# Where the weights start in SBUF: a shift of 0 to 96 bytes for each projection of a transformer block

## The chip, the cores and the metric

The kernel runs on one core of a Trainium2 chip. The metric is the device time of one execution in microseconds (us), as the median of several runs. The profile is of one execution of its own; its engines are TensorE (PE, and PEld for its weight loads), VectorE (DVE), ScalarE (ACT), GpSimd (POOL) and SyncE (SP, which issues DMAs).

## The reference

One block of a transformer on 256 tokens of 1024 features, in float32: a mixer and a feed-forward part, each behind a root-mean-square norm. The mixer joins 512 columns of attention (8 heads of 64, one block of 256 keys, so plain causal attention with a relative bias) with 512 of a gated causal convolution of 31 taps.

```python
u = rms_norm(h, mix_norm_g[l])
proj = u @ w_in[l]                                   # 1024 -> 5 * 512
q, k, v, glu_a, glu_g = jnp.split(proj, splits, axis=-1)
attn_out = moba_attention(heads(q), heads(k), heads(v), rel_bias)
conv_out = conformer_conv(glu_a, glu_g, ...)          # a * sigmoid(g), 31 taps, layer norm, silu
h = h + jnp.concatenate([attn_out, conv_out], -1) @ w_out[l]
u = rms_norm(h, ffn_norm_g[l])
h = h + (jax.nn.silu(u @ w_gate[l]) * (u @ w_up[l])) @ w_down[l]   # 2816 wide
return rms_norm(h, final_norm_g)
```

## The kernel before

Each large product is made of three matmuls on float32r operands. A weight tile raw (128 partitions x 1024 columns, 4 KB a partition) is loaded by SP; ScalarE casts it to the upper part wh, VectorE subtracts to get the rest, wl; x times its gain is cut the same way into uh and ul, the halves of u2. Then wh with uh, wh with ul and wl with uh are added in PSUM. The division by the norm is done behind the matmuls.

`high` allots wh and wl for each half n of a part, from the pool `wts` with 9 buffers for each of the tags raw (6), wh and wl. The parts' names begin with a letter: a (a and gate of the convolution), qk, v, o (output), g and u (gate and up, two 256-column halves side by side), d (down).

A matmul has a stationary operand, which a weight load (LDWEIGHTS, 128 columns) puts into the array, and a moving one. In the stages a, qk and o the weights are stationary and u2 (in o the mixer's result mh, ml) moves, 256 columns at a time. In v and gate/up, u2 is stationary and the weights move, 512 columns at a time; in down fh and fl (the feed-forward values) are stationary and the weights move. So each matmul reads one slice of a weight tile and one slice of another tile at the same time as the weight load of the next one.

Counts: a and gate 192 (`a_mm`, tiles pa and pg), queries and keys 192 (`qk_mm`, `mm3`, pqk), values 48 (`v_mm`, pv), output 192 (`o_part`, py), gate/up 528 (`up_mm`, pf), down 252 and 24 narrower ones at the end (`down`, pd and pe): 1428 of these matmuls.

The order of the work is written out by hand: PROGRAM lists the steps of the mixer, and the loop over 11 groups g at the end of the kernel those of the feed-forward part. Everything is kept in program order on each engine. The stages stand in this order: a0 and a1 (a and gate), with the sum of squares of x (`rs`: ps_x) among them; then queries and keys, attention's scores, the convolution (pc, in plain float32) and values interleaved; then output with the layer norm of the convolution's result among it (`norm`, parts 1, 2, 6, 3, 7, 4, 5); then gate/up and down in turn.

Tiles lie in SBUF one behind another in the order in which pools and tiles are made, each rounded up to 32 bytes. mhalf, of which two columns are used, is made first with 24 floats (96 bytes), so xs and u2 start 96 bytes past a multiple of 128. The 16 spare floats of pv put ones and ident at 0 and, further on, every raw, wh and wl at 96 past a multiple of 128. accx (96 past) and rbt (32 bytes) stand first in the pool w1; behind them the mixer's tiles, mh and ml among them, start at a multiple of 128. In the pool w2 the feed-forward part's tiles, fh and fl among them, start at 96 past one.

Of the kernel before, what the change touches and what calls it, by code (L numbers as in the profile page):

```python
# [10 lines left out]
F32 = mybir.dt.float32  # L11
F32R = mybir.dt.float32r
AF = mybir.ActivationFunctionType
ALU = mybir.AluOpType

P = 128
S = 256
D = 1024
KD = D // P
H = 8  # L20
HD = 64
NB = 32
TAPS = 31
CC = 4
# [6 lines left out]
ZN = 384  # L31
HW = 1024
# [4 lines left out]
FINE = ("a0_0", "a0_4")  # L37
COPY_V = (("a0_0", 0), ("a0_0", 1))
WARM = 9

PROGRAM = """
ld.a1_0 a0.0 pz a0.1 a0.2 a0.3 zs zd ld.a1_1 a0.4 a0.5 a0.6 a0.7 ld.qk0
# [13 lines left out]
PV_N = PV_FOLD + 32  # L56
# [3 lines left out]
def block_kernel(ctx, tc, xT, w_in, w_out, w_gu, w_down, pvec, gfin, relb, hot, out):  # L60
    nc = tc.nc
    const = ctx.enter_context(tc.tile_pool(name="const", bufs=1))
    wts = ctx.enter_context(tc.tile_pool(name="wts", bufs=9))
# [3 lines left out]
    w1 = ph1.enter_context(tc.tile_pool(name="w1", bufs=1))  # L67
# [3 lines left out]
    def mm(*args, **kw):  # L71
        return tc.keep_in_program_order(nc.tensor.matmul(*args, **kw))  # L72
# [12 lines left out]
    act, vec, pool, sync = (InOrder(e) for e in (nc.scalar, nc.vector, nc.gpsimd, nc.sync))  # L85

    def bank(i, name):
        return psum.tile([P, 512], F32, tag=f"b{i}", name=name)
# [17 lines left out]
    def pieces(name):  # L106
        n = HW // 2 if name in FINE else HW
        return [(i, slice(j, j + n)) for i in range(2) for j in range(0, HW, n)]
# [12 lines left out]
    def take(name):  # L121
        if name[0] in "gud" and name not in ("g0", "u0", "g1"):
            while order and len(raws) < 1 + LOOK:
                fetch(order[-1][2])
        return raws.pop(name)
# [5 lines left out]
    def high(name, i):  # L131
        if i == 0:
            raw = take(name)
            upper[name] = []
            parts[name] = []
            for n in range(2):
                wh = wts.tile([P, HW], F32R, tag="wh", name=f"wh_{name}_{n}")
                wl = wts.tile([P, HW], F32R, tag="wl", name=f"wl_{name}_{n}")
                parts[name].append((wh, wl))
                upper[name] += [(raw[n], wh, wl, c) for m, c in pieces(name) if m == n]  # L140
        raw, wh, wl, c = upper[name][i]
        if (name, i) in COPY_V:
            vec.tensor_copy(wh[:, c], raw[:, c])
        else:
            act.copy(wh[:, c], raw[:, c])
        made.add((name, i))
# [3 lines left out]
    def split(name, i=None):  # L150
        for n in range(len(pieces(name))) if i is None else (i,):
            if (name, n) not in made:
                high(name, n)
            raw, wh, wl, c = upper[name][n]
            vec.tensor_sub(wl[:, c], raw[:, c], wh[:, c].bitcast(F32))
# [10 lines left out]

    mhalf = const.tile([P, 24], F32, name="mhalf")
    xs = const.tile([P, KD, S], F32, name="xs")  # L170
    u2 = const.tile([P, KD, 2, S], F32R, name="u2")
    uh, ul = u2[:, :, 0], u2[:, :, 1]
    pv = const.tile([P, PV_N + 16], F32, name="pv")
    ones = const.tile([P, P], F32, name="ones")
    ident = const.tile([P, P], F32, name="ident")
    warm = const.tile([P, 1], F32, name="warm")
    accx = w1.tile([P, S], F32, name="accx")
    rbt = w1.tile([NB + 1, H], F32, name="rbt")
    hot_s = w1.tile([NB + 1, ZN], F32, name="hot_s", tag="lg", bufs=2)
    upad = [w1.tile([P, 2 * UW + 4], F32, name=f"upad{i}", tag="pts", bufs=4) for i in range(2)]  # L180
    ustk = []
    wstk = [w1.tile([P, 8 * Q, 32], F32, name=f"wstk{i}", tag="wstk", bufs=2) for i in range(2)]
    invc = w1.tile([P, P], F32, name="invc")
    vec.memset(warm, 0.0)
    act.dma_start(pv[:, 0:PV_T], pvec[:, 0:PV_T])
    act.activation(warm, warm, AF.Sigmoid)
# [3 lines left out]
        sync.dma_start(xs[:, k], xT[:, k * S : (k + 1) * S])  # L190
    pool.memset(ones, 1.0)
    pool.dma_start(hot_s, hot)
    pool.dma_start(rbt[0:NB, :], relb)
    wm = bank(4, "wm")
    for i in range(WARM):
        mm(wm[:, 0:P], ones, ones, start=i == 0, stop=i == WARM - 1)
    pool.memset(ident, 0.0)
    pool.affine_select(out=ident, in_=ident, compare_op=ALU.not_equal, fill=1.0, base=0,
                       pattern=[[-1, P]], channel_multiplier=1)
    pool.memset(mhalf, -0.5)  # L200
    pool.memset(rbt[NB : NB + 1, :], 1.0)
    for t in upad:
        pool.memset(t[:, 0 : TAPS - 1], 0.0)
        pool.memset(t[:, TAPS - 1 + S : UW + TAPS - 1], 0.0)
        pool.memset(t[:, UW + TAPS - 1 + S :], 0.0)
    pool.memset(invc, 1.0 / (CC * P))
    pool.dma_start(pv[:, PV_T:PV_N], pvec[:, PV_T:])

    col = lambda lo, i: pv[:, lo + i : lo + i + 1]
# [11 lines left out]
    def rstd(acc, n, eps, name, b):  # L221
        ps = bank(b, f"ps_{name}")
        for t in range(2):
            mm(ps[:, t : t + 1], acc[:, t * P : (t + 1) * P], ones[:, 0:1], start=True, stop=True)
        ms = const.tile([P, 2], F32, name=f"ms_{name}")
        vec.tensor_scalar(ms, ps[:, 0:2], 1.0 / n, eps, op0=ALU.mult, op1=ALU.add)
        rc = const.tile([P, 2], F32, name=f"rc_{name}")
        pool.tensor_tensor(rc, ms, mhalf[:, 0:2], op=ALU.pow)
        dg = const.tile([P, S], F32, name=f"dg_{name}", tag="dg")
        for t in range(2):  # L230
            vec.tensor_scalar(dg[:, t * P : (t + 1) * P], ident, rc[:, t : t + 1], None, op0=ALU.mult)
        return rc, dg

    def wide(dg, name, b):
        pb = bank(b, f"pb_{name}")
        mm(pb[:, :S], ones, dg, start=True, stop=True)
        return pb
# [22 lines left out]
    cv = lambda c: cacc[:, c]  # L260
# [75 lines left out]
    def scale_x():  # L336
        xn["c"], xn["d"] = rstd(accx, D, RMS_EPS, "x", 5)
# [16 lines left out]
    pzs = []  # L354

    def bias_mm():
        pzs.append(bank(6, "pz"))
        mm(pzs[0][0:H, 0:ZN], rbt, hot_s, start=True, stop=True)

    def bias_copy():  # L360
        act.copy(zs, pzs[0][0:H, 0:ZN])
# [120 lines left out]
    s4 = w1.tile([P, 2, S], F32, name="s4")  # L482
    ln = {}

    def norm(part):
        if part == 1:
            vec.tensor_add(s4[:, 0], s4[:, 0], s4[:, 1])
        elif part == 2:
            pm = bank(2, "pm")
            mm(pm[:, :S], invc, s4[:, 0], start=True, stop=True)  # L490
            for c in range(CC):
                vec.tensor_sub(cv(c), cv(c), pm[:, :S])
        elif part == 6:
            csq.append(w1.tile([P, CC, S], F32, name="csq", tag="wstk", bufs=2))
            for c in range(CC):
                act.activation(cw(c), cv(c), AF.Square)
        elif part == 3:
            vec.tensor_add(s4[:, 0], cw(0), cw(1))
            vec.tensor_add(s4[:, 1], cw(2), cw(3))
            vec.tensor_add(s4[:, 0], s4[:, 0], s4[:, 1])  # L500
        elif part == 7:
            _, ln["dg"] = rstd(s4[:, 0], CC * P, LN_EPS, "ln", 4)
        elif part == 4:
            ln["r"] = wide(ln["dg"], "ln", 5)
        else:
            for c in range(CC):
                vec.tensor_mul(cv(c), cv(c), ln["r"][:, :S])
                act.activation(cw(c), cv(c), AF.Silu, scale=col(PV_LG, c), bias=col(PV_LB, c))
                act.copy(mix[0][:, 4 + c], cw(c))
            for c in range(CC):  # L510
                vec.tensor_sub(mix[1][:, 4 + c], cw(c), mix[0][:, 4 + c].bitcast(F32))


    acch = const.tile([P, S], F32, name="acch")

    def finish(m):
        assert len(done) == KD - 3
# [7 lines left out]
    def a0(k):  # L525
        high(f"a0_{k // 4 * 4}", k % 4)
        upper_u(k, PV_G1)
        lower_u(k, PV_G1)
        split(f"a0_{k // 4 * 4}", k % 4)
        a_mm(0, k, f"a0_{k // 4 * 4}", k % 4 * 512)  # L530

    ops = {"ld": fetch, "zd": bias_out, "bd": bias_in, "ud": stack_out, "us": stack_in, "h": high, "w": split, "rb": row_scale, "pz": bias_mm, "zs": bias_copy, "vt": v_out, "rs": scale_x,
           "a0": a0, "a1": a1, "glu": glu, "qk": qk_mm, "qo": qk_out, "sc": score, "t": logits, "n": normed, "fl": flip,
           "fo": flip_out, "v": v_mm, "pv": pv_mm, "mo": mix_out, "l": norm, "o": o_mm, "f": finish, "c": conv,
           "co": conv_out, "cw": conv_weights, "ct": conv_taps, "hs": lambda m: sumsq(acch, xs[:, m], m, "h"),
           "sq": lambda k: sumsq(accx, xs[:, k], k, "x"), "g": lambda m: lower_u(m, PV_G2)}
# [96 lines left out]
    for k in range(KD):  # L633
        for t in range(2):
            up_mm(0, t, k)
        if k == 5:
            rc2, _ = rstd(acch, D, RMS_EPS, "h", next(spare))
            split("u1")
# [38 lines left out]
    a, b = FG - 2, FG - 1  # L677
    for t in range(2):
# [22 lines left out]
        ms = w2.tile([P, 2], F32, name=f"fms{t}")  # L701
        for n, (lo, hi) in enumerate(((512, 768), (768, 1024))):
# [5 lines left out]
            if n == 0:  # L708
# [4 lines left out]
                                 op0=ALU.mult, op1=ALU.add, accum_out=ms[:, 1:2])  # L713
# [97 lines left out]
```

## Time and profile before

| | us |
|---|---|
| median of 3 runs | 298.7 (298.55 to 298.9) |
| the profiled execution | 298.79 |
| its span (first to last instruction of the profile) | 297.0 |
| TensorE busy in the span | 289.4 (97%) |
| VectorE, ScalarE, GpSimd busy | 203.9, 149.7, 44.3 |

The page gives busy times of each engine and a chain of work followed back from the end. Matmuls overlap: one lasts longer than the time from its start to the start of the next, so the busy time of a group is less than its count times its mean. The chain in order of time gives the start and length of each piece with the count of matmuls in it, and the quotient is the time from start to start.

### The profile page before, as it was taken

Reading aid. Unit: us, or ns where it says so; the run is one execution under the profiler, and the core shown is the slowest. Engines: PE = TensorE matmul, PEld = TensorE weight load, DVE = VectorE, ACT = ScalarE, POOL = GpSimd, SP = SyncE. Lnnn points to the kernel's source line nnn. Section 1 sums busy time; section 2 is a strip of 40 time slices with the busy share of each in tenths; the row PEclk is TensorE's granted clock in tenths of the full one; section 3 lists DMA queues with packets and bytes.
Section 4 is the critical chain, followed back from the end, with each engine's and each line's share of the span. In section 5 each row is a group of like instructions: output and inputs, shape, how many; then the busy total and the mean of one; then the engine's idle time right before and its main releaser. Section 6 shows DMA issues by size and latency. Waiting matters only on the chain.

```text
span 297.0 us, 4763 instructions
## 1 busy us (share of the span) xinstructions
PE 289.4 (97%) x1750; PEld 246.9 (83%) x1750; DVE 203.9 (69%) x373; ACT 149.7 (50%) x251; POOL 44.3 (15%) x83
## 2 busy tenths in 40 slices
PE   8999999999999999999999999999999999999991
PEld 7999986988689998888888888888888888888880
DVE  2877999888988688867875738291847456321884
ACT  2984564354583768826555445271717263402531
POOL 4000000000000000124131303320421313130000
PEclk9999999999999999999999999999999999999996
DMA  6999779936227445797997968979694959520012
GB/s 182 344 406 335 251 170 261 382 94 195 74 73 225 142 144 200 244 354 228 307 348 168 310 166 275 303 259 374 222 282 134 297 144 311 165 71 0 1 68 75
DMA packets 21624, 63.73 MB, mean 215 GB/s; under 512 B 3117, under 2 KB 5701, under 8 KB 21600
## 3 DMA queue, kind: packets, MB, share of 16 engines
q1 hardware_dynamic: 18176, 54.80, 57.2%
q0 software_dynamic: 2992, 8.08, 9.8%
q10 hardware_dynamic: 432, 0.54, 0.5%
q8 instruction: 14, 0.23, 0.3%
q14 instruction: 10, 0.08, 0.1%
HBM read 58.08 MB, written 5.32 MB: 213 GB/s over the span
## 4 chain that ended last, share of the span: by engine, by line
PE 92%; issue 2%; DMA 2%; DVE 1%; SPq 0%; POOLq 0%; POOL 0%; ACT 0%; DVEq 0%
PE pf L72 40%; PE pd L72 17%; PE pqk L72 8%; PE py L72 8%; PE pv L72 4%; PE pa L72 4%; PE pg L72 4%; PE pc L72 4%; DMA xs<-in_xT 2%; PE ps L72 1%; PE pt L75 1%; PE po L72 1%; DVE ht L83 1%; SPq L83 0%; DVE hg L83 0%
## 5 line engine op out<-in xcount | busy, mean ns | idle before, releaser
L72 PE MATMUL pf<-wh_u,u 128*128 128x512 f32 x176 | 56.2, 390 | 0.0
L72 PE MATMUL pf<-wh_g,u 128*128 128x512 f32 x176 | 55.9, 389 | 0.0
L83 DVE TENSOR_TENSOR ff<-fs,pf 128x256 f32<-128x256 f32 x22 | 9.1, 420 | 53.4 <-ACT fs L83 53.4
L83 ACT ACTIVATE fs<-pf,rc_h 128x256 f32<-128x256 f32 x22 | 10.4, 476 | 65.9 <-PE pf L72 65.4
L72 PEld LDWEIGHTS pf<-wh_u,u 128*128 128x128 f32 x176 | 33.0, 188 | 6.8
L72 PEld LDWEIGHTS pf<-wh_g,u 128*128 128x128 f32 x176 | 33.0, 188 | 6.8
L72 PE MATMUL pf<-wl_g,u 128*128 128x512 f32 x88 | 34.2, 389 | 0.0
L72 PE MATMUL pf<-wl_u,u 128*128 128x512 f32 x88 | 34.2, 389 | 0.0
L72 PE MATMUL pd<-wh_d,fh 128*128 128x512 f32 x84 | 32.9, 391 | 0.0
L72 PE MATMUL pd<-wh_d,fl 128*128 128x512 f32 x84 | 32.7, 390 | 0.0
L72 PE MATMUL pd<-wl_d,fh 128*128 128x512 f32 x84 | 32.7, 389 | 0.0
L83 DVE TENSOR_TENSOR wl_u<-raw_u,wh_u 128x1024 fp32r<-128x1024 f32 x22 | 26.6, 1223 | 7.5 <-ACT wh_u L83 7.4
L83 POOL DMA_DIRECT2D fb<-fd x40 | 23.2, 588 | 46.5 <-DMA fd<-fv 22.8
L83 ACT CAST wh_u<-raw_u 128x1024 fp32r<-128x1024 f32 x22 | 22.9, 1053 | 12.5 <-PE pf L72 9.2
L83 DVE TENSOR_TENSOR wl_g<-raw_g,wh_g 128x1024 fp32r<-128x1024 f32 x22 | 25.9, 1221 | 2.0 <-ACT wh_g L83 2.0
L83 DVE TENSOR_TENSOR wl_d<-raw_d,wh_d 128x1024 fp32r<-128x1024 f32 x22 | 25.6, 1205 | 0.5 <-ACT wh_d L83 0.5
L72 PE MATMUL pqk<-u,wh_qk 128*128 128x256 f32 x128 | 23.6, 286 | 0.0
L83 ACT CAST wh_g<-raw_g 128x1024 fp32r<-128x1024 f32 x22 | 22.0, 1049 | 0.0
L83 ACT CAST wh_d<-raw_d 128x1024 fp32r<-128x1024 f32 x22 | 21.9, 1045 | 0.0
L72 PEld LDWEIGHTS pqk<-u,wh_qk 128*128 128x128 f32 x128 | 20.0, 192 | 0.4 <-issue 0.3
L72 PEld LDWEIGHTS pf<-wl_u,u 128*128 128x128 f32 x88 | 16.5, 188 | 3.4
L72 PEld LDWEIGHTS pf<-wl_g,u 128*128 128x128 f32 x88 | 16.5, 188 | 3.4
(156 smaller groups left out, 558.4 us busy)
## 6 DMA issues: line engine op xcount, KB each, us to landing
raw_g<-in_w_gu SPq DMA_DIRECT2D x22, 512.0 KB, 5.6
raw_u<-in_w_gu SPq DMA_DIRECT2D x22, 512.0 KB, 7.0
raw_d<-in_w_down SPq DMA_DIRECT2D x22, 512.0 KB, 4.7
raw_qk<-in_w_in SPq DMA_DIRECT2D x8, 512.0 KB, 7.2
raw_o<-in_w_out SPq DMA_DIRECT2D x8, 512.0 KB, 4.2
fd<-fv POOLq DMA_DIRECT2D x10, 256.0 KB, 4.0
fb<-fd POOLq DMA_DIRECT2D x40, 64.0 KB, 5.8
ustk<-ud SPq DMA_DIRECT2D x8, 288.0 KB, 5.7
```

The lines of the kernel that those rows point to most:

```text
L72: return tc.keep_in_program_order(nc.tensor.matmul(*args, **kw))
L75: return tc.keep_in_program_order(nc.tensor.transpose(o, i, ident))
L83: return lambda *a, **k: tc.keep_in_program_order(f(*a, **k))
```

## The change

Every slot of wh and wl becomes 32 floats (128 bytes) longer, and the part lies in it s floats from the start: 24 (96 bytes) for a and gate, 16 (64 bytes) for queries, keys, values and down, 8 (32 bytes) for output, 0 for gate and up. mhalf moves behind ident and shrinks to 8 bytes, pv's padding from 16 to 8 floats, rbt is widened to 128 bytes and accx and acch become one tile, acc, in the first pool. With that xs, u2, raw, all slots of wh and wl, fh and fl start at a multiple of 128 bytes; mh and ml stay at one. hg and fsq, at the end, start 32 bytes past one.

The tile invc (all 1/512) goes: the mean over the convolution's channels is now made with ones, and the division is done in the subtraction.

```diff
+SHIFT = {"a": 24, "q": 16, "o": 8, "v": 16, "d": 16}
+
...
             for n in range(2):
-                wh = wts.tile([P, HW], F32R, tag="wh", name=f"wh_{name}_{n}")
-                wl = wts.tile([P, HW], F32R, tag="wl", name=f"wl_{name}_{n}")
+                s = SHIFT.get(name[0], 0)
+                wh, wl = (wts.tile([P, HW + 32], F32R, tag=w, name=f"{w}_{name}_{n}")[:, s : s + HW] for w in ("wh", "wl"))
                 parts[name].append((wh, wl))
...
-    mhalf = const.tile([P, 24], F32, name="mhalf")
+
     xs = const.tile([P, KD, S], F32, name="xs")
     u2 = const.tile([P, KD, 2, S], F32R, name="u2")
     uh, ul = u2[:, :, 0], u2[:, :, 1]
-    pv = const.tile([P, PV_N + 16], F32, name="pv")
+    pv = const.tile([P, PV_N + 8], F32, name="pv")
     ones = const.tile([P, P], F32, name="ones")
     ident = const.tile([P, P], F32, name="ident")
+    mhalf = const.tile([P, 2], F32, name="mhalf")
     warm = const.tile([P, 1], F32, name="warm")
-    accx = w1.tile([P, S], F32, name="accx")
-    rbt = w1.tile([NB + 1, H], F32, name="rbt")
+    accx = acch = const.tile([P, S], F32, name="acc")
+    rbt = w1.tile([NB + 1, 32], F32, name="rbt")
...
-    invc = w1.tile([P, P], F32, name="invc")
...
-    pool.memset(invc, 1.0 / (CC * P))
...
-            mm(pm[:, :S], invc, s4[:, 0], start=True, stop=True)
+            mm(pm[:, :S], ones, s4[:, 0], start=True, stop=True)
             for c in range(CC):
-                vec.tensor_sub(cv(c), cv(c), pm[:, :S])
+                vec.scalar_tensor_tensor(cv(c), pm[:, :S], -1.0 / (CC * P), cv(c), op0=ALU.mult, op1=ALU.add)
...
-
-    acch = const.tile([P, S], F32, name="acch")
```

The left-out lines of the diff take the first 8 columns of the wider rbt where it is used, and all of the narrower mhalf.

No instruction changes its place. On VectorE, in the mixer's layer norm (s is s4, cacc the convolution's result, pm its mean, ml the lower part of the mixer's result), before:

```order
L83 TENSOR_TENSOR s_148<-s_148 128x256
L83 TENSOR_SCALAR vt<-pv_838,rc_x 128x512
L83 TENSOR_TENSOR cacc<-cacc,pm 128x256 x4
L83 TENSOR_TENSOR ml<-po_1127,mh 128x256
L83 TENSOR_TENSOR ml<-po_1136,mh 128x256
L83 TENSOR_TENSOR ml<-po_1148,mh 128x256
```

and after:

```order
L85 TENSOR_TENSOR s_146<-s_146 128x256
L85 TENSOR_SCALAR vt<-pv_835,rc_x 128x512
L85 SCALAR_TENSOR_TENSOR cacc<-pm,cacc 128x256 x4
L85 TENSOR_TENSOR ml<-po_1124,mh 128x256
L85 TENSOR_TENSOR ml<-po_1133,mh 128x256
L85 TENSOR_TENSOR ml<-po_1145,mh 128x256
```

The four subtractions of the mean are another form of instruction, in the same place. On GpSimd, near the start of the kernel (pv holds the constants), before:

```order
L83 MEMSET upad_80 128x32
L83 MEMSET upad_80 128x6
L83 MEMSET invc 128x128
L83 DMA pv<-in_pvec 128x156
L83 DMA zd<-zs 8x384
L83 TENSOR_TENSOR rc_x<-ms_x,mhalf 128x2
```

and after:

```order
L85 MEMSET upad_80 128x32
L85 MEMSET upad_80 128x6
L85 DMA pv<-in_pvec 128x156
L85 DMA zd<-zs 8x384
L85 TENSOR_TENSOR rc_x<-ms_x,mhalf 128x2
```

The load of the second part of pv stands one instruction further forward. The rows of TensorE, ScalarE and SP are the same but for the names accx, acch and invc.

## Rows read from the trace of the kernel before

**Rows 1.** Page: busy time, granted clock in 40 slices, chain by engine.

```profile
PE 289.4 (97%) x1750; PEld 246.9 (83%) x1750; DVE 203.9 (69%) x373; ACT 149.7 (50%) x251; POOL 44.3 (15%) x83
...
PEclk9999999999999999999999999999999999999996
...
PE 92%; issue 2%; DMA 2%; DVE 1%; SPq 0%; POOLq 0%; POOL 0%; ACT 0%; DVEq 0%
```

**Rows 2.** Chain that ended last, in order of time: start us, us, what.

```profile
24.03 0.59 PE ps_x L72 x4
...
28.03 0.24 PE pa L72 x2
...
54.11 2.88 PE pqk L72 x24
...
95.51 14.24 PE py L72 x120
...
148.35 10.88 PE pf L72 x48
...
159.23 5.44 PE pd L72 x24
```

**Rows 3.** Tiles pqk, pg, py: count, shortest/median/longest ns, first and last start.

```profile
L72 PEld LDWEIGHTS pqk<-u,wh_qk x128: 186/192/192, 30.6 to 69.4; 128*128 128x128 f32 x128
...
L72 PE MATMUL pqk<-u,wl_qk x64: 278/283/286, 31.0 to 69.7; 128*128 128x256 f32 x64
...
L72 PE MATMUL pg<-u,wh_a x64: 274/283/415, 5.4 to 30.1; 128*128 128x256 f32 x64
...
L72 PEld LDWEIGHTS py<-ml,wh_o x64: 187/188/193, 85.9 to 109.2; 128*128 128x128 f32 x64
L72 PE MATMUL py<-ml,wh_o x64: 277/281/285, 86.1 to 109.4; 128*128 128x256 f32 x64
```

**Rows 4.** Timeline: start us, us, engine, operation [idle time before it <- releaser].

```profile
4.86 0.77 PE L72 MATMUL pa<-u,wh_a 128*128 128x256 f32 x2
...
24.01 0.52 PEld L72 LDWEIGHTS ps_x<-ones,accx 128*128 128x128 f32 x4 [0.19 <-DVE accx L83]
...
86.54 0.76 DVE L83 TENSOR_TENSOR ml<-po,mh 128x256 fp32r<-128x256 f32 x2 [1.07 <-ACT mh L83]
```

**Rows 5.** Stretches: busy us (count) of PE, PEld, DVE, ACT, POOL; clock, DMA.

```profile
30.00:40.00 10.00, 10.00 (x86) 9.86 (x86) 9.67 (x15) 5.71 (x8) 1.17 (x2) 1.00 0.84 235
40.00:50.00 10.00, 10.00 (x135) 6.67 (x132) 9.68 (x34) 5.40 (x18) 0.00 (x0) 1.00 0.82 192
```

**Rows 6.** Tiles pf, pd, pv: matmuls of 512 columns, columns as in rows 3.

```profile
L72 PE MATMUL pf<-wh_g,u x176: 389/389/395, 109.6 to 267.6; 128*128 128x512 f32 x176
...
L72 PE MATMUL pf<-wl_u,u x88: 387/389/390, 115.3 to 272.9; 128*128 128x512 f32 x88
...
L72 PE MATMUL pd<-wh_d,fl x84: 389/389/398, 143.2 to 288.7; 128*128 128x512 f32 x84
...
L72 PE MATMUL pv<-wh_v,u x32: 388/392/499, 56.8 to 81.4; 128*128 128x512 f32 x32
...
L72 PE MATMUL pv<-wl_v,u x16: 387/389/398, 57.1 to 81.2; 128*128 128x512 f32 x16
```

**Rows 7.** Tiles cacc, pe, invc, wstk, acch: operations of VectorE, GpSimd and ScalarE.

```profile
L83 DVE TENSOR_TENSOR cacc<-cacc,pm x4: 414/416/422, 83.2 to 84.2; 128x256 f32<-128x256 f32 x4
...
L83 DVE SCALAR_TENSOR_TENSOR ht<-pe,rc_h,ht x4: 483/483/484, 284.4 to 290.5; 128x256 f32<-128x256 f32 x4
...
L83 POOL MEMSET invc<- x1: 210/210/210, 3.7 to 3.7; 128x128 f32 x1
...
L83 DVE TENSOR_TENSOR wstk<-pv x2: 1749/1749/1749, 37.4 to 57.6; 128x1536 f32<-128x1536 f32 x2
...
L83 ACT ACTIVATE acch<-xs x1: 410/410/410, 112.6 to 112.6; 128x256 f32<-128x256 f32 x1
```

**Rows 8.** DMA issues: count, KB each, median us from issue to landing.

```profile
out<-hg SPq DMA_DIRECT2D x4, 128.0 KB, 2.2
```

More of the change, by code (lines that the diff above doesn't have):

```diff
@@ L192, in block_kernel @@
     pool.dma_start(hot_s, hot)
-    pool.dma_start(rbt[0:NB, :], relb)
+    pool.dma_start(rbt[0:NB, 0:H], relb)
     wm = bank(4, "wm")
@@ L200, in block_kernel @@
     pool.memset(mhalf, -0.5)
-    pool.memset(rbt[NB : NB + 1, :], 1.0)
+    pool.memset(rbt[NB : NB + 1, 0:H], 1.0)
     for t in upad:
@@ L227, in rstd @@
         rc = const.tile([P, 2], F32, name=f"rc_{name}")
-        pool.tensor_tensor(rc, ms, mhalf[:, 0:2], op=ALU.pow)
+        pool.tensor_tensor(rc, ms, mhalf, op=ALU.pow)
         dg = const.tile([P, S], F32, name=f"dg_{name}", tag="dg")
@@ L357, in bias_mm @@
         pzs.append(bank(6, "pz"))
-        mm(pzs[0][0:H, 0:ZN], rbt, hot_s, start=True, stop=True)
+        mm(pzs[0][0:H, 0:ZN], rbt[:, 0:H], hot_s, start=True, stop=True)
     def bias_copy():
```

## The prediction

> **What bounds the kernel now.** I read the page's busy shares and chain first: TensorE is busy for 97% of the 297.0 us span, 92% of the chain that ended last is its matmuls, and its granted clock is 1.00 (2.4 GHz) up to the last slice [rows 1]. So a change pays only in the time from one matmul's start to the next. The reader finds that step in the chain in order of time, by dividing a piece by its count [rows 2]. Queries and keys: 24 matmuls of 256 columns in 2.88 us, 120.0 ns each. The a and gate stage: two in 0.24 us, the same. Output: 120 in 14.24 us, 118.67 ns. Gate/up: 48 of 512 columns in 10.88 us, 226.67 ns; down: 24 in 5.44 us, again 226.67 ns.
>
> At 2.4 GHz 120.0 ns is 288 clocks and 226.67 ns is 544: in both cases the columns and 32 clocks more. The excess goes by the matmul, not by the column, and each matmul comes with one load of 128 weights beside it. The output stage has an excess of only 28.8 clocks. What sets it apart in the code is the place of its operands: in all other stages u (or fh, fl) and the weights both start 96 bytes past a multiple of 128, in the output stage the moving tiles mh and ml start at 0 and the weights at 96. I call the start of the weights less the start of the other operand, modulo 128, their distance: 0 everywhere before, 96 in the output stage. The durations tell the same: 283 ns at the median with loads of 192 ns at distance 0, 281 and 188 at distance 96 [rows 3].
>
> **The change, part by part.** Its instructions are those of before but for one memset and four vector operations; what it moves is addresses. The distances after are: a and gate 96 (from 0), queries and keys 64 (from 0), output 32 (from 96), values and down 64 (from 0), gate/up 0 as before, with both operands moved from 96 to 0.
>
> a and gate, 192 matmuls, take the very distance that the output stage has in the trace. 120.0 to 118.67 ns is 1.33 ns, times 192 0.26 us. But 144 of them stand ahead of the sum over x (the matmul ps_x), and there TensorE already waits 0.19 us for VectorE's last addition to accx [rows 4]; what 144 x 1.33 = 0.19 us would save makes that wait longer. The 48 behind it keep 48 x 1.33 = 0.06 us.
>
> Queries and keys, 192 matmuls, go to 64, which no row has. Their own rows are at 0 and the output stage's at 96; 64 is nearer to 96, so I take 1.33 ns again, 0.26 us. From both sides: the 256-column matmuls of these stages last between 274 ns (one of pg) and 286 ns (one of pqk), away from the first after a break, against 283 [rows 3]: 9 ns less to 3 ns more, 192 times, -1.7 to +0.6 us. VectorE is 97% busy from 30 to 50 us [rows 5], so a faster TensorE would there wait for wl_qk sooner; the trace has no such wait yet, and I take nothing off for it.
>
> Output, 192 matmuls, 96 to 32: between the rows of 0 and of 96, which differ by 1.33 ns in the bad direction at most if 32 acted as 0; I take 0. Both ends: 277 to 285 ns against 281 [rows 3], 4 ns either way, -0.8 to +0.8 us.
>
> Values (48) and down (252), 0 to 64: the trace has 512-column matmuls at distance 0 only. In long runs they all last 389 ns; behind breaks, where the values stand, they last 387 to 398 ns [rows 6]. As bounds that is 2 ns less to 9 ns more, times 300: -0.6 to +2.7 us. The nearest row is the unbroken run itself, 226.67 ns in down and gate/up alike, whichever of many slots, slices and tiles they read; I take 0 and keep both ends. The 24 pe matmuls at the end belong to the same distance and weigh 24 x 1.3 = 0.03 us either way.
>
> Gate/up, 528 matmuls: distance kept, both starts moved. I take 0, since down, with fh, fl and weights elsewhere in memory, has the same step. Should the start itself matter, the rows of pf give 387 to 395 ns against 389 [rows 6]: -1.1 to +3.2 us.
>
> At this place a rule of the Trainium skill speaks against any effect. The row first: the output stage's step is 1.33 ns shorter, with loads of 188 instead of 192 ns [rows 2, 3]. SBUF — State Buffer, Who interferes with whom, gives TensorE two independent read ports, one for the moving operand and one for the weights, and says that TensorE never waits on another reader. By that rule no placement of weights against u can change a step, and this term is 0 instead of -0.32 us. The trace speaks against it, though weakly: stages differ in more than their addresses.
>
> The rest lies beside other work. The subtraction of the mean becomes four scalar_tensor_tensor: the form with a PSUM operand lasts 483 ns where the present tensor_tensor lasts 416, so 4 x 0.07 = 0.27 us more on VectorE [rows 7]. Behind them VectorE waits 1.07 us for ScalarE's mh [rows 4], which takes this up. Without that cover it would cost 0.27 us at most. The memset of invc, 0.21 us on GpSimd at 3.75 us, goes, and the load of the convolution's constants behind it is issued that much earlier; the convolution's weights are built from them at 37.4 us, and nobody waits [rows 7]. Sharing acc puts the second sum's first write behind matmuls that ended at 24.6 us; it comes at 112.6 us [rows 2, 7]. Tiles for raw weights and x move from 96 to 0 too; nothing in the trace prices that, and only the first loads, up to the first matmul at 4.86 us [rows 4], are uncovered: I take 0. hg moves to 32 past 128; the stores of it land 2.2 us after their issue [rows 8], and I take 0 with 0.1 us either way, a twentieth of that.
>
> Sum: -0.06 - 0.26 = -0.32 us. The profiled execution took 298.79 us (span 297.0 and 1.8 around it), the median of the runs is 298.7. From the median: 298.4 us.
>
> **The rivals.** First, nothing comes of it: addresses do not matter, or what does is only whether the distance is a multiple of 64 bytes, so that queries, values and down stay as they are. For it: down and gate/up agree to 0.01 ns in spite of different tiles. Against it: the output stage. Time: 298.7, or 298.6 with the 0.06 of a and gate.
>
> Second, faster by much more: the new distances bring the short rows throughout. Queries and keys at 277 ns (the output stage's shortest) save 6 x 192 = 1.15 us, output at 277 saves 4 x 192 = 0.77 us, the 48 of a 0.3 us, values and down at 387 save 0.6 us, together 2.8 us. That every matmul takes the shortest row is the end of it; half, 1.4 us, is my price: 297.3 us. For it: loads of 187 ns and matmuls of 277 ns do occur. Against: in the output stage they come only in turn with 283 ns.
>
> Third, the start of the moving operand counts, not the distance: mh and ml at 0 are what helps the output stage, and u and gate/up weights at 0 get the same 1.33 ns. Then queries and keys 192, a 48 and gate/up 528 save 768 x 1.33 = 1.0 us: 297.7 us. Against: with 512 columns no row shows a gain.
>
> Fourth, slower: down and values lose the steady step. At distance 0 they settle on 226.67 ns; at 64 they may run as the values do behind breaks, 392 ns at the median of wh_v against 389 [rows 6]. 300 x 3 ns = 0.9 us more, less the 0.3 us of the forecast: 299.3 us. It decides from about 1 ns a matmul in down on, and is slower beyond what can be told from 3 ns on. For it: 398 ns is farther from 389 than 387 is. Against: it needs 64 to be worse than 0, and in the output stage a distance other than 0 did no harm.
>
> **How the numbers follow.** Forecast 298.4 us, chance 0.30; no effect, 0.20; shorter rows throughout, 0.28; start of the moving operand, 0.10; lost steady step, 0.12. A measurement of this kernel tells about 0.2% (0.6 us) from no change. So faster has 0.38, the same 0.50, slower 0.12. The range for 8 in 10 reaches from 297.0, past the price of the second and third rival but short of the end of 2.8 us, to 299.3, the fourth; the unknown bounds of down lie above it to +2.7 us and are left out with the rest.
>
> **What would show it.** In the chain of the changed kernel: a and gate at 0.237 us for two, 24 of queries and keys in 2.85 us, 120 of output in 14.24, 48 of gate/up in 10.88, 24 of down in 5.44. The median loads of pqk at 188 ns instead of 192 would show the output stage's state there. TensorE's wait for acc ahead of ps_x should be 0.3 to 0.4 us. I am wrong if down's 24 leave 5.44 us by over 0.05 either way, if gate/up's 48 leave 10.88 (then the start itself counts), or if queries and keys stay at 2.88 (then 64 acts as 0).

## The result, and the profile after

The change makes the kernel slower: 300.93 us at the median of 6 runs (300.38 to 301.94) against 298.8 us for the kernel before on the same chip (298.55 to 299.65). The ratio is 1.0068, with an interval from 1.0046 to 1.0091. The profiled execution took 301.18 us with a span of 299.4. 298.4 us was forecast, and the result lies above the range.

The page of the changed kernel, busy time and chain by engine, answers to [rows 1]:

```profile
PE 291.4 (97%) x1750; PEld 245.7 (82%) x1750; DVE 203.2 (68%) x373; ACT 149.0 (50%) x251; POOL 44.0 (15%) x82
...
PE 87%; DMA 4%; issue 2%; DVE 2%; ACT 2%; SPq 1%; POOLq 0%; POOL 0%; DVEq 0%
```

TensorE is 2 us longer busy with the same 1750 matmuls. Its share of the chain fell because the first 24 us are now put down to DMA, ScalarE and VectorE; that costs nothing, as the next view shows. The chain in order of time (start us, us, what), beside [rows 2]:

```profile
24.00 0.61 PE ps_x L74 x4
...
28.21 0.23 PE pg L74 x2
...
30.79 8.28 PE pqk L74 x72
...
49.98 2.75 PE pqk L74 x24
...
94.56 14.24 PE py L74 x120
...
148.03 11.11 PE pf L74 x48
...
159.14 5.55 PE pd L74 x24
```

The reader divides pieces again. Queries and keys: 2.75 us for 24 in this row, 114.6 ns a matmul instead of 120 (2.75 to 2.83 us in the last four rows). Output: 14.24 us as before. Gate/up: 11.11 us for 48, 231.4 ns instead of 226.67. Down: 5.55 for 24, 231.3 instead of 226.67. The starts show where the balance turns: output's piece starts 0.95 us earlier than before (94.56 against 95.51), gate/up's piece only 0.32 us earlier (148.03 against 148.35), and the span ends 2.4 us later. So the mixer won about 0.95 us up to there, and what follows, the feed-forward part above all, lost about 3.35.

The single tiles (shortest/median/longest ns), beside [rows 3, 6]:

```profile
L74 PEld LDWEIGHTS pqk<-u,wh_qk x128: 187/188/192, 30.5 to 68.5; 128*128 128x128 f32 x128
...
L74 PE MATMUL pqk<-u,wl_qk x64: 276/276/342, 30.9 to 68.7; 128*128 128x256 f32 x64
...
L74 PE MATMUL pf<-wh_g,u x176: 387/392/399, 108.6 to 269.8; 128*128 128x512 f32 x176
...
L74 PE MATMUL pf<-wl_u,u x88: 388/395/397, 114.4 to 275.1; 128*128 128x512 f32 x88
...
L74 PE MATMUL pd<-wh_d,fl x84: 388/393/399, 142.8 to 291.1; 128*128 128x512 f32 x84
```

The median of queries and keys went from 283 to 276 ns, that of their loads from 192 to 188. The feed-forward matmuls have lost the one value, 389, at which nearly all of them stood; they now spread over 387 to 399 (477 behind a break) with a median of 392 to 395, wh and wl, gate/up and down alike.

What all of them share is the length of the slots, 4224 bytes instead of 4096. It was a whole number of times 512 before, so every wh and every wl lay at the same place modulo 512, and so did u, fh and fl (all at 224, by the addresses of the built program). After the change neighbouring slots lie 128 bytes apart modulo 512, and since 9 x 4224 = 74 x 512 + 128, each slot of wl lies 128 past the slot of wh with the same number. The two parts of a tile mostly get slots of the same number (73 of the 94 tiles; in the others wl lies 0 or 256 past wh). "Distance" from here on is the weights' start less the other operand's, modulo 512. In gate/up it was 0 for every matmul before; now it goes through 0, 128, 256 and 384.

### The profile page after: what moved, and what is told of

It is laid out like the page before. It is cut to its first block, busy times and chain, and to the rows that moved or that the text cites. A ratio compares the mean times of both kernels' runs of the same rounds, so it can differ in the third digit from the quotient of the medians.

```text
span 299.4 us, 4761 instructions
## 1 busy us (share of the span) xinstructions
PE 291.4 (97%) x1750; PEld 245.7 (82%) x1750; DVE 203.2 (68%) x373; ACT 149.0 (50%) x251; POOL 44.0 (15%) x82
## 4 chain that ended last, share of the span: by engine, by line
PE 87%; DMA 4%; issue 2%; DVE 2%; ACT 2%; SPq 1%; POOLq 0%; POOL 0%; DVEq 0%
PE pf L74 41%; PE pd L74 18%; PE py L74 8%; PE pqk L74 7%; DMA raw_a<-in_w_in 4%; PE pv L74 4%; PE pc L74 4%; PE ps L74 1%; SPq L85 1%; PE pt L77 1%; ACT wh_a L85 1%; PE pa L74 1%; PE pg L74 1%; PE po L74 1%; DVE ht L85 1%
## 5 line engine op out<-in xcount | busy, mean ns | idle before, releaser
L74 PE MATMUL pf<-wh_u,u 128*128 128x512 f32 x176 | 56.9, 393 | 0.0
L74 PE MATMUL pf<-wh_g,u 128*128 128x512 f32 x176 | 56.6, 393 | 0.0
L74 PE MATMUL pqk<-u,wh_qk 128*128 128x256 f32 x128 | 22.7, 280 | 0.0
L74 PEld LDWEIGHTS pqk<-u,wh_qk 128*128 128x128 f32 x128 | 19.4, 188 | 0.4 <-issue 0.3
```

## The experiments

A row of matmuls is called locked where all its steps are equal (113.33, 120.00 or 226.67 ns). Elsewhere the steps differ from one matmul to the next, and the number is their mean.

**long_slots_all_96.** The changed kernel with its slots, but without the shifts, and all starts at 96 modulo 128.

```diff
-SHIFT = {"a": 24, "q": 16, "o": 8, "v": 16, "d": 16}
+SHIFT = {}
+    mhalf = const.tile([P, 24], F32, name="mhalf")   # first tile, as before
-    pv = const.tile([P, PV_N + 8], F32, name="pv")
+    pv = const.tile([P, PV_N + 16], F32, name="pv")
```

> The changed kernel with no shift inside the slots and mhalf and pv padded as before, so that u, fh, fl and every slot start 96 bytes past a multiple of 128 again; only the longer slots stay (4224 bytes for 4096). Three theories of the lost steady step of the 512-column matmuls. Slots: 9 slots of 4224 put wl 128 bytes past wh modulo 512 and spread the distance to u over multiples of 128, and that alone unsettles them: 48 of gate/up in 11.1 us and 24 of down in 5.55, as in the changed kernel, time about 301 us. Start: moving both operands from 96 to 0 did it: 10.88 and 5.44 us again, time about 298.7. Distance modulo 128 (that of the prediction): all distances are 0, so 10.88 and 5.44, and 2.88 us for 24 of queries and keys.

Measured: 302.06 us, ratio 1.0106 [1.0080, 1.0133]. Its chain:

```profile
51.44 2.85 PE pqk L74 x24
...
149.88 11.11 PE pf L74 x48
...
160.98 5.57 PE pd L74 x24
```

Gate/up 231.5 ns, down 232.1, queries and keys 118.8: with every start back at 96 and every distance modulo 128 at 0, the feed-forward part is as slow as after the change, and the mixer has lost its gain: from ps_x (at 25.00 us, 1 us late in this execution) to output's piece it takes 71.32 us, against 71.48 before and 70.56 after the change. The slots cost the loss; the shifts brought the gain.

**short_slots_all_0.** The changed kernel with slots of 4096 bytes and no shifts, so all starts at 0 modulo 128.

```diff
-SHIFT = {"a": 24, "q": 16, "o": 8, "v": 16, "d": 16}
+SHIFT = {}
-    ... wts.tile([P, HW + 32], ...)[:, s : s + HW]
+    ... wts.tile([P, HW], ...)[:, s : s + HW]
```

> The changed kernel with slots of 4096 bytes and no shift: u, weights, fh and fl all start at a multiple of 128, the rest of the change stays. Slots: all distances between u and weights are the same modulo 512 again, so 48 of gate/up in 10.88 us and 24 of down in 5.44, queries and keys 2.88 for 24, time about 298.7 us. Start: 11.1 and 5.55 us, time about 301.

Measured: 299.11 us, ratio 1.0006 [0.9991, 1.0022]. Its chain:

```profile
50.42 2.87 PE pqk L74 x24
...
95.34 14.38 PE py L74 x120
...
148.34 10.88 PE pf L74 x48
...
159.22 5.44 PE pd L74 x24
```

Gate/up and down are back at 226.67 ns to the last digit though both their operands have moved from 96 to 0: the start itself doesn't count. Output went from 118.67 to 119.8 (120.00 in unbroken rows); its distance is 256 here and was 352 before.

**u_64_apart_in_mixer.** The kernel before; u2 gets 128 floats more and is read at two places, 448 bytes on in the mixer (weights less u: 64) and at its old place in the feed-forward part.

```diff
-    u2 = const.tile([P, KD, 2, S], F32R, name="u2")
+    u2 = const.tile([P, KD * 2 * S + 128], F32R, name="u2")
+    uv = {PV_G1: u_at(112), PV_G2: u_at(0)}   # views that start so many floats on
```

> The kernel before, slots of 4096 bytes; only u is placed anew: the tile is 512 bytes longer, in the mixer u starts 448 bytes further on (weights less u is 64 modulo 512), in the feed-forward part where it was (0). Slots: queries and keys and a and gate take the short step that queries and keys have in the changed kernel (113.3 to 115 ns, 24 in 2.75 us instead of 2.88), gate/up and down keep 10.88 and 5.44; some 384 x 5 ns = 1.9 us less, of which a and gate's first 144 may be lost to the wait for the sum over x: 297.0 to 297.9 us. The values at distance 64 in uniform slots are not known: 226 to 233 ns. Start: the same distance with u at 32 past a multiple of 128 need not help, 2.8 to 2.9 us for 24 of queries and keys.

Measured: 298.1 us, ratio 0.9974 [0.9949, 0.9999]. Its chain:

```profile
50.57 2.83 PE pqk L72 x24
...
54.05 2.74 PE pqk L72 x24
...
148.04 10.88 PE pf L72 x48
```

Distance 64 makes the gain without long slots, but not always: one row of queries and keys runs at 114.2 ns a matmul (113.33 in its unbroken part), another at 117.9. The one is locked, the other nearly so (117 to 119 ns); which of them a row falls into changes from row to row and, as the runs below show, from kernel to kernel. The time lies just above the range expected (297.0 to 297.9). A part of what queries and keys gained went into a wait: TensorE stood 0.31 us ahead of the first convolution matmuls, for the reason that mixer_and_output_64 shows below.

**scan_of_down_distances.** The kernel before with u of the feed-forward part 448 bytes on (gate/up at 64), and fh and fl in longer slots, 16 bytes further in each group, so that down's groups have distances of 0, -16, -32 ... -112, then -128, 256 and 0.

```diff
+STEP = (0, 4, 8, 12, 16, 20, 24, 28, 32, 64, 0)
-    acts[g] = [w2.tile([P, 2, 2, P], ...)]
+    acts[g] = [w2.tile([P, 4 * P + 128], ...)[:, STEP[g] : STEP[g] + 4 * P] ...]
```

> The kernel before with slots of 4096 bytes; in the feed-forward part u starts 448 bytes further on (gate/up at distance 64 modulo 512), and fh and fl lie in slots of 2560 bytes at a step that grows with the group: 0, 16, 32, ... 112, 128, 256 bytes for groups 0 to 9. A map, no time wanted: the step of down's 24 matmuls by distance. Slots: every group settles on one step, since all distances are uniform within it; 226.67 ns at 0, 128 and 256 if the period is 128 or less; values of 512 columns and a multiple of 16 clocks (220.0, 226.67, 233.3 ns) where a group locks. Start or distance modulo 128: 128 and 256 as 0, 64 as in the changed kernel (231 to 233 ns). Gate/up at distance 64: 231 ns if distance alone decides, 226.67 if only uniformity does.

Measured, in one run: 300.93 us. Its chain, one piece of gate/up and the pieces of down at -16, -32, -48, -96 and -112:

```profile
148.41 10.99 PE pf L73 x48
...
159.40 5.44 PE pd L73 x24
...
175.83 5.60 PE pd L73 x24
...
192.42 5.60 PE pd L73 x24
...
242.19 5.62 PE pd L73 x24
...
258.81 5.59 PE pd L73 x24
```

Down holds 226.67 at 0 and -16, and jumps to 233 (5.60) at -32; from there to -112 it stays between 232 and 234. The last groups, broken by other work, have a median of 232 ns at -128 and 227 at 256. Gate/up at a uniform 64 runs at 229.0, unlocked. So it is not enough that all distances are equal, and 256 does the same as 0.

**shifts_without_long_slots.** The kernel before with the changed kernel's distances modulo 128 for queries, keys, values, output and down (a and gate at 64 too), made on the other operand's side.

```diff
+    uv = {PV_G1: u_at(112), PV_G2: u_at(0)}
+    t = w1.tile([P, KD * S + 80], ...)                # mh, ml: t[:, 80:]
+    acts[g] = [w2.tile([P, 4 * P + 128], ...)[:, 112 : 112 + 4 * P] ...]
```

> The kernel before with its short slots of 4096 bytes (all weights' parts at one place modulo 512), and the distances of the changed kernel made on the other side: u of the mixer read 448 bytes further on, which puts queries, keys, values and a and gate 64 past it; mh and ml so that output is at 32; fh and fl so that down is at 64; gate/up stay at 0. Theory 'long slots' (most of the loss is the slots' spread modulo 512): gate/up 226.67 ns, queries and keys 113 to 118 ns, down 231 to 234 ns by its shift of 64 as in the scan, so 252 x 5.5 ns = 1.4 us lost there and 0.7 to 1.2 us won in the mixer: 298.7 to 300.0 us. Rival 'the shifts themselves lose' (the loss of 2.2 us comes from the new distances and not from the slots): as slow as the changed kernel, 300.4 to 301.5 us, with gate/up off 226.67.

Measured: 298.52 us, ratio 0.9997 [0.9979, 1.0016]. Its chain:

```profile
148.72 10.88 PE pf L72 x48
...
159.60 5.49 PE pd L72 x24
```

Without the long slots the same shifts cost nothing on balance; the time lies 0.2 us under the range expected. Gate/up is locked, and down at a uniform 64 loses 0.05 us in 24 (228.9 ns), under half of the 5.5 ns a matmul that were expected from the scan. The expectation had taken the scan's rows at -64 for 64: at 64 the scan had gate/up, with 229.0 ns, and that is what down does here.

**lower_parts_128_on.** The kernel before with one gap of 128 bytes between the slots of wh and of wl.

```diff
+                if not n and name == "a0_0":
+                    wts.tile([P, 32], F32R, tag="gap", name="gap", bufs=1)
                 wl = wts.tile([P, HW], F32R, tag="wl", ...)
```

> The kernel before with one gap of 128 bytes between the slots of the upper parts and those of the lower ones: in gate/up the two matmuls with wh keep distance 0, the one with wl has 128; in down wl has 0 and the two with wh have 384. Nothing is spread over slots. Theory 'each matmul by its own distance': a third of gate/up leaves 226.67 ns by 6 ns or so (233 at 384 in the scan of down), two thirds of down do: 176 x 6 + 168 x 6 = 2.1 us, 300.5 to 301.2 us, and the wh matmuls of gate/up keep 226 to 227. Theory 'one broken distance unlocks the row': all matmuls of gate/up at 229 to 233, whichever part they read: 301 to 302.5 us. Rival 'only the spread over slots hurts': 226.67 throughout, 298.5 to 299.3 us.

Measured: 303.37 us, ratio 1.0149 [1.0119, 1.0179], the slowest of all. Its chain:

```profile
148.86 11.20 PE pf L72 x48
...
160.06 5.50 PE pd L72 x24
```

Gate/up runs at 233.4 ns throughout: the two matmuls in three that kept distance 0 are as slow (232.8 at the mean) as the one at 128 (234.2). The step is not a matter of each matmul's own distance. One broken distance in three is enough to unlock the row, and 528 x 6.7 ns = 3.5 us go by it. The time lies above the range given for that (301 to 302.5 us). Down, where two in three are at 384 and one at 0, runs at 229: it loses less with two broken distances in three than gate/up does with one, and no run shows why.

**distances_32_64_256.** Short slots; a, gate, queries and keys at 32, output at 64, gate/up at 256 (views of u2 at 120 and 64 floats, mh and ml 72 floats on).

> A scan in short slots: u in the mixer placed so that a, gate, queries, keys and values are at 32; mh and ml so that output is at 64; u in the feed-forward part so that gate/up are at 256. Theory 'period of 256 bytes': gate/up 226.67 ns as at 0; output 113.3 ns locked, or 117.7, as queries and keys at 64; at 32 queries and keys between 113 and 120 ns, unlocked. Rival 'period of 512': gate/up 229 to 234 ns, and 64 does for output something else than for queries and keys, since mh and ml have rows of 1024 bytes and not of 2048.

Measured, in one run: 297.8 us. Its chain:

```profile
50.57 2.85 PE pqk L72 x24
...
95.14 13.62 PE py L72 x120
...
147.35 10.88 PE pf L72 x48
```

Gate/up at 256 is locked at 226.67. Output at 64 is 113.5 (113.33 in unbroken rows), 0.62 us less in this piece than before [rows 2]. Queries and keys at 32 run unlocked at 118.8.

**mixer_and_output_64.** The version that the runs so far point to: short slots, mixer and output at 64, the feed-forward part at 0.

```diff
+    uv = {PV_G1: u_at(112), PV_G2: u_at(0)}
+    t = w1.tile([P, KD * S + 72], ...)                # mh, ml: t[:, 72:]
```

> A version meant to beat both: short slots, queries, keys, values, a and gate at 64 by the place of u, output at 64 by the place of mh and ml, gate/up and down at 0 as before. Theory 'distance': output's 192 matmuls at 113.3 ns instead of 118.67 add 1.0 us to the gain of 0.7 us that the place of u gave: 296.9 to 297.4 us; if output sticks at 117.7 ns, 297.9. Rival 'nothing from output' (its train with another operand layout does not lock): 298.0 to 298.3 us.

Measured: 297.85 us, ratio 0.9964 [0.9947, 0.9982]: faster than both kernels, by less than was hoped. The 297.9 us of the expectation stood for output at 117.7 ns; output did better, and that the time agrees is luck. Its chain:

```profile
54.97 2.83 PE pqk L72 x24
...
95.99 13.62 PE py L72 x120
...
148.18 10.88 PE pf L72 x48
```

Output gives its 0.62 us here too. Queries and keys fell into 117.8 ns in most rows, and what a, gate and queries gained ended in a wait. The timeline row of the first convolution matmuls ([idle time before <- releaser]), and what the trace has on the four loads of ustk that they read:

```profile
44.30 2.80 PE L72 MATMUL pc<-ustk,wstk 128*32 128x256 f32 x48 [1.61 <-DVE rs L83]
...
L83 SPq DMA_DIRECT2D ustk<-ud x4: 329/424/431, 36.2 to 37.5; - x4
...
DMA to landing us min/median/max: 3.5/5.2/6.6
```

The convolution reads ustk, which comes back from DRAM. The last of the four loads is issued at 37.5 us and lands at 44.1, 0.2 us ahead of the first convolution matmul. In the kernel before they were issued 1.1 us earlier:

```profile
L83 SPq DMA_DIRECT2D ustk<-ud x4: 330/427/443, 35.1 to 36.4; - x4
...
DMA to landing us min/median/max: 3.4/5.1/6.2
```

There the last landed at 42.6 us, and TensorE came to it at 43.4. The VectorE operation that the timeline names feeds no convolution. So TensorE came early, ustk came late, and TensorE stood 1.61 us. The waits of 0.31 us in u_64_apart_in_mixer and of 0.49 us in shifts_without_long_slots are the same: in both the convolution begins 0.2 us behind the last landing (43.2 and 43.9 us).

**long_slots_pairs_256.** The changed kernel with a gap of 128 bytes more between the slots of wh and of wl, so that wl lies 256 past wh in most tiles; the slots themselves still spread.

```diff
+                if gap:
+                    wts.tile([P, 32], F32R, tag="gap", name="gap", bufs=1)
```

> The changed kernel with one more gap of 128 bytes between the slots of the upper and of the lower parts, so that wl lies 256 past wh modulo 512 instead of 128. The slots stay long, so over the slots gate/up's distance still goes 0, 128, 256, 384, but the three matmuls of a step now agree modulo 256. Theory 'a row keeps 226.67 ns when all its distances are 0 modulo 256': the slots at 0 and 256 hold 226 to 228 ns except just behind a slot at 128 or 384, and those at 128 and 384 lie at 229 to 234: gate/up 229.5 at the mean and 299.4 to 300.4 us in all. Rival 'the pair of wh and wl alone matters': 226.67 ns throughout, 298 to 298.8 us. Rival 'any spread over the slots costs the whole row': gate/up 231 ns as in the changed kernel, 300.4 to 301.5 us.

Measured: 301.45 us, ratio 1.0085 [1.0058, 1.0113]. Its chain:

```profile
147.31 11.07 PE pf L74 x48
...
158.38 5.56 PE pd L74 x24
...
180.54 11.04 PE pf L74 x48
```

Gate/up 230.0 to 230.6 ns. Upper parts at distance 0 and lower parts at 256, which mostly belong to the same tiles, have come down to 228.3 and 227.8 ns at the mean (232.7 and 230.8 in the changed kernel); those at 128 and 384 stay at 231 to 233. But upper parts at 256 went up, from 229.2 to 231.3. The time is in the rival's range and not below the changed kernel's. So the run supports the theory of 256 bytes by a part of its steps only; that gate/up is bad by the pair of wh and wl alone it rules out.

**distances_80_48_128.** Short slots; a, gate, queries and keys at 80, output at 48, gate/up at a uniform 128 (views of u2 at 108 and 96 floats, mh and ml 76 floats on).

> A scan in short slots, as the one of 32, 64 and 256: a, gate, queries and keys at 80, output at 48, gate/up at a steady 128, down at 0. Theory 'period of 256 bytes, and 64 is the middle of the quick place': gate/up at a steady 128 is the worst place half way round, 229 to 234 ns; 80 and 48, 16 to either side of 64, still lock at 113.3 ns, as 16 below 0 did for down. Rival 'only multiples of 64 lock': 80 and 48 at 116 to 119 ns, unlocked. Rival 'what hurts 512 columns is the change between distances, not 128 itself': gate/up 226.67 ns.

Measured, in one run: 302.72 us. Its chain:

```profile
51.39 2.85 PE pqk L72 x24
...
96.31 14.29 PE py L72 x120
...
149.99 11.16 PE pf L72 x48
```

Gate/up at a uniform 128 is 232.5 ns, as bad as any mixture: 128 itself is the bad place. Queries and keys at 80 and output at 48 run unlocked at 119: the quick place at 64 is narrow.

**scores_before_conv.** mixer_and_output_64, with the scores of heads 2 and 3 ahead of the first convolution matmuls.

```diff
-qo.1 c.0.0 h.v0.0 n.0 ct.0.1.3 sc.1 t.1
+qo.1 h.v0.0 n.0 ct.0.1.3 sc.1 c.0.0 t.1
```

> The version with mixer and output at 64, and in the program's table the scores of heads 2 and 3 (sc.1) ahead of the first convolution matmuls (c.0.0). In the profile of mixer_and_output_64 TensorE stood 1.61 us ahead of the convolution, whose operand ustk was still on its way from DRAM, while the 0.86 us of sc.1 lay behind. Theory 'the mixer's gain is lost in that wait': TensorE waits 0.7 us for the vector multiplication that makes qk, does the scores, and finds ustk landed: 0.2 to 0.9 us less than mixer_and_output_64, 297.0 to 297.7 us. Rival 'the wait is chance of one profiled execution, and ustk is mostly in time': the wait for qk is new, and it is 0.3 to 0.7 us slower, 298.2 to 298.6 us.

Measured: 297.89 us, ratio 0.9963 [0.9947, 0.9980]: the same as without the move. TensorE's timeline:

```profile
44.43 0.93 PE L72 MATMUL ps<-qk 64*128 64x128 f32 x8 [0.90 <-DVE qk L83]
45.29 4.96 PE L72 MATMUL pc<-ustk,wstk 128*32 128x256 f32 x88
```

It waits 0.90 us for qk, as both theories had it, and the convolution then follows without a wait; what one side gains the other takes. Neither theory's time came. In this execution ustk had landed at 42.5 us, in time; of the four profiled executions with u at 64 in the mixer it was late in three. How often it is late in the others stays open.

## Why the prediction was wrong

The step that failed is "Gate/up, 528 matmuls: distance kept, both starts moved. I take 0", and with it the 0 taken for values and down. The prediction reckoned distances modulo 128, from two stages of before, and looked only at the offset inside the slot. Of the slot's new length it took no notice: 32 floats are 0 modulo 128 bytes, and so seemed to leave everything in place. Modulo 256 and 512 they do not. Gate/up's distance was not kept; it became a mixture. By the rows of the chain that is 0.23 us for 48 and 2.3 us over all pieces of gate/up, and 0.11 to 0.13 us for each 24 of down, 1.0 us over all. The sum of 3.3 us agrees with the 3.35 us between the starts. Of two kernels without any shift, long_slots_all_96 makes the loss and short_slots_all_0 does not.

The loss itself was in the bounds (-1.1 to +3.2 us for gate/up, -0.6 to +2.7 for down), but it was cut off the range as a case of "the start itself". The condition written for it, gate/up's 48 leaving 10.88, came true, as did the one for down; the reason beside the first, that then the start counts, did not: the starts moved in short_slots_all_0 and nothing followed. The fourth rival had the effect right (the steady step of 226.67 is lost) and its size for a third of the matmuls only, with down's shift as its cause; that shift alone costs 2.25 ns a matmul (shifts_without_long_slots), 0.6 us over down.

Queries and keys: forecast -0.26 us for 192, from the output stage's step; by the pieces of the chain it was -0.88 us (the first 72 in 8.28 us, 115.0 ns each, instead of 8.64), near the 1.15 us that the second rival gave this stage. The term had the right sign by luck, from a row that was not at the same place: 352, the output stage's distance before, is not locked, 64 is. That shortest rows of 276 ns could hold in every matmul stood only in a rival.

a and gate: two in 0.23 us, near the forecast 0.237, and TensorE's wait ahead of ps_x became 0.3 us, as forecast. With queries and keys that makes the 0.95 us of the mixer. The wait (engine, tile, line <- releaser: us in total, times, longest):

```profile
PE ps_x L74 <- DVE acc L85: 0.3, 1, 0.3
```

Output: forecast 0, measured 14.24 us for 120 again, though its distances spread over 32, 160, 288 and 416. None of these locked, nor had 352; the reason given, that 32 lies between two rows, had no part in it, and the 0 came true by luck.

The subtraction of the mean: forecast 0.07 us more for each of the four operations, and hidden. The extra time isn't there:

```profile
L85 DVE SCALAR_TENSOR_TENSOR cacc<-pm,cacc x4: 415/416/425, 82.2 to 83.2; 128x256 f32<-128x256 f32 x4
```

416 ns at the median, as the tensor_tensor of [rows 7]; the 483 ns there belong to a form whose scale is a column of a tile. The edit would have been free without cover.

The rule that was weighed, SBUF — State Buffer, Who interferes with whom, in the Trainium skill, by which TensorE never waits on another reader, was read as giving no change of step from any placement. In gate/up, lower_parts_128_on moves only the lower parts, by 128 bytes, and makes it 3.0% slower (11.20 against 10.88 us for 48), so here the measurement decides against that reading of it.

## What to carry over

An offset inside a buffer is half of an address; the buffer's length is the other half, and with rotating slots it decides where each later tile lies. Before tiles are padded or shifted, list every operand's start modulo a few powers of two, for every slot, not for the first. A run of matmuls that keeps one step throughout is a state worth guarding: a change of placement can break it (128 bytes did, 256 did not), and the step in the chain shows it at once.

## What the runs showed of the hardware

With float32r operands the step from matmul to matmul depends on where the weights lie against the other operand in SBUF. For 512 moving columns (weights moving) it is 226.67 ns at distances of 0, -16 and 256 bytes, 229 at 64, and 232 to 234 at 128 and from -32 to -112. In gate/up a mixture of two at 0 and one at 128 runs wholly at 233.4; in down one of two at 384 and one at 0 runs at 229, so a mixture does not follow from its shares. For 256 moving columns (weights stationary) it is 120.00 ns at 0 and 256, 113.33 or a second steady value near 117.7 at 64, and 118 to 119.5 unlocked at 32, 48, 80 and 352. At the granted clock of 1.00 (2.4 GHz) the locked steps are 272, 288 and 544 clocks.

What in the chip makes it so no run shows. It stays open too which of its two values a row at 64 takes; output took 113.33 in all three kernels that had it there, queries and keys either.
